# Attention weights requested a piece per half step, and an up projection of seven half-block products, in a hybrid encoder block

## The chip, the core and the metric

The kernel runs on one core of a Trainium2 chip. The metric is the device time in microseconds (us), the median of the runs. The engines have short names: PE multiplies matrices (PEld is its weight load, which overlaps), DVE is the vector engine, ACT the scalar engine, POOL is GpSimd, SP issues most DMAs. SBUF is the on-chip memory, PSUM holds what PE adds up, in banks of 128x512 float32.

## The reference

One layer on x of 1024 tokens by 1024 channels, float32. Two mixers read the normalised input; the second half is a gated feed-forward with a convolution of width 3 over the tokens:

```
proj = rmsnorm(x) @ w_in          # mLSTM q,k,v,o,gates; attention q,k,v; gates ga, gb
h_a  = mLSTM(both directions)     # 4 heads, chunks of 128 tokens
p    = softmax(q k^T)             # 8 heads of 2 x 64; weights p0 - lam * p1
h_b  = rmsnorm((p0 - lam*p1) @ v)
x    = x + (sigmoid(ga)*(h_a @ p_a) + sigmoid(gb)*(h_b @ p_b)) @ w_o
u    = conv3(rmsnorm(x) @ w_up) + conv_b      # 1024 x 5632
a, g = split(u)
x    = x + (gelu(g) * a) @ w_down             # 2816 x 1024
```

## The kernel before

**Products.** PE works in a short float32 format, so every matrix is split into a high half (a cast on ACT, L81) and a low half (a subtraction, L82, on DVE unless the caller names POOL), and each product is three matmuls: high by high, high by low, low by high (`mm3`, L112 to L114).

**Weights.** `wgran` brings 128x1024 numbers into `wraw`, a pool of one buffer (`NR = 1`), and splits them into `whi` and `wlo` (four buffers each). `load_w` does that for two such granules at once, where a set is asked for. All these DMAs are issued by SP.

**Order.** The program is written as Python loops; a scheduler with its own model of durations puts each engine's instructions into one fixed order, and semaphores hold an instruction until its inputs are there. An engine that waits holds all that stands behind.

**Stages**, by their times in the profile: the mLSTM to 445 us; attention, 445 to 1285; merge with p_a, p_b and w_o to 1547; feed-forward to the end.

**Attention** walks 32 steps (8 heads x 4 pairs of query blocks). `soft` (L645 to L657) makes scores, row maxima, exponentials `p` (ACT, L651) and subtracts the second softmax (DVE, L657). `av` transposes the weights (L677), splits them into `wTh` and `wTl`, and multiplies with v. Between these matmuls `filler(h, n)`, called for each of eight half steps n of a head, puts projections for later heads: q and k (`qk_piece`, L573 to L605), v, and the gates ga, gb (`gates`, ends with a tanh into `tg`, L162). It asks for the whole weight set at n = 2 (v, or the next gate set) and at n = 6 (q and k, two heads on). `kst` is a copy of the keys into the other half of the partitions, by DMA. `PRO` gate pieces are made before the first step, `LAST` says how many in the last head, `PA` how many blocks of h_a @ p_a are made there early.

**Norm and feed-forward.** `norm_transpose` (L206 to L217) scales a token half, transposes it on PE and splits it into `xn2`. For each of 22 column blocks j of 128, `up(j)` loads w_up's columns for a and g, multiplies (2 x 2 halves of tokens x 8 blocks of rows x 3 matmuls = 96 of 128x512) into PSUM tile `big`, and convolves from there: one ACT step (L936) and two of DVE (L937, L938); then gelu (L944), the product a*g (L946) and its split. After each pair of j, `down` multiplies the pair of before with w_down (96 matmuls) and adds into the eight resident tiles of x (L962, 16 adds of 128x512 a pair).

Of the kernel before, what the change touches and what calls it, by code (L numbers as in the profile page):

```python
# [10 lines left out]
F32 = mybir.dt.float32  # L11
F32R = mybir.dt.float32r
AF = mybir.ActivationFunctionType
ALU = mybir.AluOpType
# [30 lines left out]
TURN1 = {1: (1,)}  # L45

# [5 lines left out]
class Kern:  # L52
# [41 lines left out]

    def load_w(self, srcs, lo_eng=None):

        gr = []
        for g in range(2):
            loads, off = [], 0
            for s in srcs:  # L100
                n = s.shape[-1]
                loads.append((
                    lambda r, o=off, n=n: r.rearrange("p (k c) -> p k c", k=4)[:, :, o:o + n],
                    s[g * 512:(g + 1) * 512].rearrange("(k p) c -> p k c", p=P)))
                off += n
            hi, lo = self.wgran(loads, lo_eng)
            gr.append((hi.rearrange("p (k c) -> p k c", k=4), lo.rearrange("p (k c) -> p k c", k=4)))
        return lambda k: (gr[k // 4][0][:, k % 4], gr[k // 4][1][:, k % 4])

    def mm3(self, ps, a, b, start, stop):  # L110
        mm = self.nc.tensor.matmul
        mm(ps, a[0], b[0], start=start, stop=False)  # L112
        mm(ps, a[0], b[1], start=False, stop=False)  # L113
        mm(ps, a[1], b[0], start=False, stop=stop)  # L114

    def proj_cm(self, ps, w, c0, x, half):
        for _ in self.proj_cm_g(ps, w, c0, x, half):
# [25 lines left out]

    def gate_w(self, gg):
        if gg not in self.gst and gg < 8:
            off = (O_GA, O_GB)[gg // 4] + (gg % 4) * 256
            self.gst[gg] = self.load_w([self.I["w_in"][0][:, off:off + 256]])

    def gates(self, count, pool, ahead=False):
        for _ in range(count):  # L150
# [25 lines left out]
    def early_ya(self, tg, wide):  # L176
        m = self.ny
        self.ny += 1
        if m % 2 == 0:
            self.wpa = self.load_w([self.I["p_a"][0][:, m * P:m * P + 256]])  # L180
        self.nc.sync.dma_start(tg, self.sig_d[0][m * P:(m + 1) * P, :])
        ps = self.big() if wide else None
        for half in range(2):
            t = slice(half * 512, half * 512 + 512)
            pv = ps[:, t] if wide else self.small(tag="pj")
            yield from self.proj_cm_g(pv, self.wpa, (m % 2) * P, self.ha, half)
            self.nc.vector.scalar_tensor_tensor(tg[:, t], tg[:, t], 1.0, pv, op0=ALU.add, op1=ALU.mult)
        self.nc.sync.dma_start(self.ya_d[m * P:(m + 1) * P, :], tg)


def rstd_pow(K, out, ss, n, scr, width):
# [297 lines left out]
def attention(K, xn, hb_d):  # L489
# [3 lines left out]
    with tc.tile_pool(name="at", bufs=1, reuse_waits="tile") as ap, ExitStack() as es:  # L493
# [44 lines left out]
            while pend:  # L538
                tick()

        def load_v(hp):
            o = Obj()
            o.w = K.load_w([w_in[:, O_AV + hp * 256:O_AV + hp * 256 + 256]], G)
# [15 lines left out]
        def load_qk(h):  # L559
            o = Obj()  # L560
            o.w = K.load_w([w_in[:, O_AQ + h * 128:O_AQ + h * 128 + 128], w_in[:, O_AK + h * 128:O_AK + h * 128 + 128]], G)
            o.q, o.k, o.st = [], [], {}
            return o

# [69 lines left out]
        def soft(o, st, j):  # L634
# [12 lines left out]
            for c_ in range(2):  # L647
                sp = sps[c_]
                V.tensor_reduce(sm[:, c_:c_ + 1], sp, op=ALU.max, axis=AX.X, negate=True)  # L649
                p_ = ap.tile([P, 1024], F32, tag=f"p{c_}", bufs=3 - 2 * c_, name=K.nm("p"))  # L650
                A.activation(p_, sp, AF.Exp, bias=sm[:, c_:c_ + 1], accum_out=sm[:, 2 + c_:3 + c_])  # L651
                pt.append(p_)
            V.reciprocal(sm[:, 4:6], sm[:, 2:4])
            V.tensor_copy(st.inv[:, j:j + 1], sm[:, 4:5])
# [80 lines left out]
                        tick()  # L735

        on = vn = None

        def is_v(h):
            return h % 2 == 1 and h + 1 < AH  # L740
# [80 lines left out]
def merge_ffn(K, ha_d, hb_d, out):  # L821
    nc, tc, I = K.nc, K.tc, K.I
    V, G, A, T = nc.vector, nc.gpsimd, nc.scalar, nc.tensor
    with tc.tile_pool(name="mf", bufs=1, reuse_waits="tile") as fp, ExitStack() as es:
# [61 lines left out]
        xn, pw = None, []  # L886

        def pair(k):
            if k % 2 == 0:
# [16 lines left out]
            for bp in range(4):  # L906
                wo_piece(w, cg, bp * 2)
        ws = [wo(2), wo(3)]
        for half in range(2):
            for i in range(2):  # L910
                if half == 1 and i == NCG:
                    sp = [g4("nxs", tag="wk") for _ in range(2)] + [g4("nxs", tag="B") for _ in range(2)]
                    xn = h2("xn2", "B")
                    norm_transpose(K, lambda blk: acc[blk], xn, g2, fp, 0, lambda x: [sp.pop(0)] * 2, pair)
                for bp in range(2):
                    wo_piece(ws[i], 2 + i, half * 4 + bp * 2)
        norm_transpose(K, lambda blk: acc[blk], xn, g2, fp, 1, lambda x: [g4("nxs")] * 2, lambda k: K.small())
        ffn(K, fp, g4, acc, xn, out)


def ffn(K, fp, g4, acc, xn, out):
    nc, tc, I = K.nc, K.tc, K.I
    V, G, A, T = nc.vector, nc.gpsimd, nc.scalar, nc.tensor
    w_up, w_dn = I["w_up"][0], I["w_down"][0]
    cw = fp.tile([P, 3, 44], F32, tag="cw", name="cw")
    cb = fp.tile([P, 44], F32, tag="cb", name="cb")
    for t in range(3):
        nc.sync.dma_start(cw[:, t, :], I["conv_w"][0][t, 0].rearrange("(k p) -> p k", p=P))
    nc.sync.dma_start(cb, I["conv_b"][0].rearrange("(k p) -> p k", p=P))

    def conv(j, w, c0):
        u = K.big()
        for half in range(2):
            K.proj_cm(u[:, half * 512:half * 512 + 512], w, c0, xn, half)
        c = g4("cv")
        A.activation(c, u, AF.Identity, bias=cb[:, j:j + 1], scale=cw[:, 1, j:j + 1])  # L936
        V.scalar_tensor_tensor(c[:, 1:], u[:, :1023], cw[:, 0, j:j + 1], c[:, 1:], op0=ALU.mult, op1=ALU.add)  # L937
        V.scalar_tensor_tensor(c[:, :1023], u[:, 1:], cw[:, 2, j:j + 1], c[:, :1023], op0=ALU.mult, op1=ALU.add)  # L938
        return c

    def up(j):
        w = K.load_w([w_up[:, j * P:(j + 1) * P], w_up[:, DFF + j * P:DFF + (j + 1) * P]])
        g = conv(NFF + j, w, P)
        A.activation(g, g, AF.Gelu_apprx_tanh)  # L944
        a = conv(j, w, 0)
        V.tensor_tensor(a, a, g, op=ALU.mult)  # L946
        hh = g4("fhh", F32R)
        hl = g4("fhl", F32R)
        K.split(hh, hl, a)
        return hh, hl  # L950

    def down(j0, hs):
        ws = [K.wgran([(lambda r: r, w_dn[(j0 + i) * P:(j0 + i + 1) * P, :])]) for i in range(2)]
        last = j0 + 2 == NFF
        for blk in range(NB):
            t = slice(blk * P, (blk + 1) * P)
            for half in range(2):
                o = slice(half * 512, half * 512 + 512)
                ps = K.small()
                for i in range(2):  # L960
                    K.mm3(ps, (hs[i][0][:, t], hs[i][1][:, t]), (ws[i][0][:, o], ws[i][1][:, o]), i == 0, i == 1)
                V.tensor_tensor(acc[blk][:, o], acc[blk][:, o], ps, op=ALU.add)  # L962
                if last and blk == NB - 1:
                    nc.sync.dma_start(out[blk * P:, o], acc[blk][:, o])
            if last and blk < NB - 1:
                nc.sync.dma_start(out[blk * P:(blk + 1) * P, :], acc[blk])

    prev = None
    for j in range(0, NFF, 2):
        hs = [up(j), up(j + 1)]  # L970
        if prev is not None:
            down(*prev)
        prev = (j, hs)
    down(*prev)


@with_exitstack
# [62 lines left out]
```

## Time and profile before

| what | value |
|---|---|
| runs | 2294.85, 2299.35, 2299.68 us |
| median | 2299.35 us |
| profiled execution | 2291.85 us, its span 2290.1 us |
| mean granted PE clock | 0.986 |
| PE busy | 96% of the span |

The span runs from the first to the last instruction that the profiler shows; times in rows count from its start. Busy counts only time in which an instruction runs. A matmul's own duration overlaps the next one's, so the cost of one in a row of matmuls is read from a window with its count. The granted clock of 1.00 is 2.4 GHz, 0.5 is 1.2 GHz.

### The profile page before, as it was taken

How to read it: one execution, taken by the hardware profiler on the slowest of the kernel's cores; microseconds unless marked ns; L12 is line 12 of the kernel's file. 1: busy time of each engine (PE TensorE's matmuls, PEld its weight loads, DVE VectorE, ACT ScalarE, POOL GpSimd, SP SyncE). 2: the span in 40 equal slices, each digit the busy share in tenths (PEclk: the TensorE clock that was granted, in tenths of full speed). 3: DMA queues.
4: the chain of work that ended last, by engine and by line, in shares of the span. 5: the costliest groups of instructions: out<-in, count | busy, mean ns of one | idle time of the engine just before them, and what ended most of it. 6: DMA issues, size and time to landing. Idle time of an engine off the chain costs nothing.

```text
span 2290.1 us, 29966 instructions
## 1 busy us (share of the span) xinstructions
PE 2197.2 (96%) x12200; PEld 1888.8 (82%) x12200; DVE 1239.5 (54%) x2020; ACT 804.1 (35%) x1429; POOL 313.8 (14%) x298
## 2 busy tenths in 40 slices
PE   7999999989999899899999999999999999999999
PEld 6888888888789789798878778997888888888887
DVE  3455252358687686787755345244444444545455
ACT  4333232245455455555545222133222221222220
POOL 0131101233133141332300010000000000000000
PEclk9999999999999999999999999999999999999999
DMA  3123222221210311202232665111111111111112
GB/s 121 40 83 98 64 55 74 77 57 35 63 43 26 79 31 37 71 21 63 52 97 70 194 166 159 63 47 47 37 56 47 47 51 42 38 54 56 45 48 83
DMA packets 171307, 150.83 MB, mean 66 GB/s; under 512 B 37304, under 2 KB 153048, under 8 KB 171168
## 3 DMA queue, kind: packets, MB, share of 16 engines
q1 hardware_dynamic: 165616, 129.17, 20.2%
q0 software_dynamic: 5552, 19.73, 2.7%
q8 instruction: 96, 1.57, 0.3%
q14 instruction: 43, 0.35, 0.0%
HBM read 117.64 MB, written 22.84 MB: 61 GB/s over the span
## 4 chain that ended last, share of the span: by engine, by line
PE 76%; DMA 10%; DVE 6%; ACT 3%; issue 3%; POOL 2%; SPq 1%; ACTq 0%; POOLq 0%; DVEq 0%
PE pj L112 8%; PE pj L113 8%; PE pj L114 7%; PE big L114 7%; PE big L112 7%; PE big L113 7%; PE sm L112 6%; PE sm L113 6%; PE sm L114 6%; DMA wraw<-in_w_in_dram 6%; PE big L645 4%; PE pt L677 2%; ACT whi L81 2%; POOL wlo L82 1%; PE cr L435 1%
## 5 line engine op out<-in xcount | busy, mean ns | idle before, releaser
L81 ACT CAST whi<-wraw 128x1024 fp32r<-128x1024 f32 x156 | 163.7, 1049 | 596.0 <-PE sm L114 207.5
L82 DVE TENSOR_TENSOR wlo<-wraw,whi 128x1024 fp32r<-128x1024 f32 x132 | 162.5, 1231 | 372.2 <-ACT whi L81 372.1
L112 PE MATMUL pj<-whi,xn 128*128 128x256 f32 x960 | 277.6, 289 | 15.5 <-ACT whi L81 15.4
L112 PE MATMUL big<-xn2h,whi 128*128 128x512 f32 x704 | 278.2, 396 | 1.0 <-ACT xn2h L216 1.0
L114 PE MATMUL big<-xn2h,wlo 128*128 128x512 f32 x704 | 279.1, 396 | 0.0
L113 PE MATMUL big<-xn2l,whi 128*128 128x512 f32 x704 | 277.2, 394 | 0.8 <-DVE xn2l L217 0.8
L113 PE MATMUL pj<-wlo,xn 128*128 128x256 f32 x960 | 276.3, 288 | 0.5 <-POOL wlo L82 0.4
L114 PE MATMUL pj<-whi,xn 128*128 128x256 f32 x960 | 276.2, 288 | 0.0
L112 PE MATMUL pj<-xn,whi 128*128 128x512 f32 x512 | 212.6, 417 | 12.6 <-ACT xn L216 5.5
L114 PE MATMUL pj<-xn,wlo 128*128 128x512 f32 x512 | 209.0, 408 | 0.0
L113 PE MATMUL pj<-xn,whi 128*128 128x512 f32 x512 | 208.8, 408 | 0.0
L112 PEld LDWEIGHTS pj<-whi,xn 128*128 128x128 f32 x960 | 185.1, 193 | 19.5 <-ACT whi L81 17.3
L113 PEld LDWEIGHTS pj<-wlo,xn 128*128 128x128 f32 x960 | 185.0, 193 | 2.9 <-POOL wlo L82 1.3
L962 DVE TENSOR_TENSOR x<-x,sm 128x512 f32<-128x512 f32 x176 | 119.6, 686 | 122.9 <-PE sm L114 122.9
L114 PEld LDWEIGHTS pj<-whi,xn 128*128 128x128 f32 x960 | 185.0, 193 | 0.8
L651 ACT ACTIVATE p<-big,smx 128x1024 f32<-128x1024 f32 x128 | 143.2, 1120 | 89.2 <-DVE smx L649 72.8
L649 DVE TENSOR_REDUCE smx<-big 128x1 f32<-128x1024 f32 x128 | 154.3, 1217 | 36.9 <-PE big L645 36.5
L645 PE MATMUL big<-kst,qst 128*128 128x512 f32 x512 | 145.5, 410 | 16.6 <-DMA kst<-kst 12.0
L113 PEld LDWEIGHTS big<-xn2l,whi 128*128 128x128 f32 x704 | 132.2, 188 | 34.0 <-DVE xn2l L217 1.1
L112 PEld LDWEIGHTS big<-xn2h,whi 128*128 128x128 f32 x704 | 132.2, 188 | 32.4 <-ACT xn2h L216 1.2
L114 PEld LDWEIGHTS big<-xn2h,wlo 128*128 128x128 f32 x704 | 132.2, 188 | 32.1
L112 PE MATMUL sm<-whi,fhh 128*128 128x512 f32 x352 | 139.4, 396 | 0.0
(255 smaller groups left out, 4408.5 us busy)
## 6 DMA issues: line engine op xcount, KB each, us to landing
wraw<-in_w_up_dram SPq DMA_DIRECT2D x88, 256.0 KB, 3.2
wraw<-in_w_in_dram SPq DMA_DIRECT2D x40, 512.0 KB, 5.3
wraw<-in_w_in_dram SPq DMA_DIRECT2D x48, 256.0 KB, 4.5
wraw<-in_w_down_dram SPq DMA_DIRECT2D x22, 512.0 KB, 3.2
x<-in_x_dram SPq DMA_DIRECT2D x16, 512.0 KB, 4.7
sig<-tg SPq DMA_DIRECT2D x32, 256.0 KB, 2.4
kst<-kst SPq DMA_DIRECT2D x64, 128.0 KB, 2.4
tgl<-sig POOLq DMA_DIRECT2D x13, 512.0 KB, 4.5
```

Of the source, the lines that this page charges most:

```text
L81: self.nc.scalar.copy(hi, src)
L82: (lo_eng or self.nc.vector).tensor_tensor(lo, src, hi.bitcast(F32), op=ALU.subtract)
L112: mm(ps, a[0], b[0], start=start, stop=False)
L113: mm(ps, a[0], b[1], start=False, stop=False)
L114: mm(ps, a[1], b[0], start=False, stop=stop)
L435: T.matmul(nps[:, :MV + 1], pm[:, t], va[:, j, :], start=True, stop=i == 0)
L645: T.matmul(sps[c_][:, half * 512:half * 512 + 512], o.q[st.qp][:, c_, t], o.k[half][:, c_, s_, :], start=s_ == 0, stop=s_ == 1)
L649: V.tensor_reduce(sm[:, c_:c_ + 1], sp, op=ALU.max, axis=AX.X, negate=True)
L651: A.activation(p_, sp, AF.Exp, bias=sm[:, c_:c_ + 1], accum_out=sm[:, 2 + c_:3 + c_])
L677: T.transpose(pt[:, kk * 256 + j * P:kk * 256 + (j + 1) * P], st.w[j][:, kb * P:(kb + 1) * P], K.ident)
L962: V.tensor_tensor(acc[blk][:, o], acc[blk][:, o], ps, op=ALU.add)
```

## The change

**Attention.** A class `Weights` splits a set's life into `load(g)`, which requests one granule, and `make(g)`, which splits it. `filler` requests the first granule at n = 0, splits it and requests the second at n = 1, splits that at n = 2 and requests the next set, and so on. `make` is told to come after `K.mark`, the latest exponential. The low halves of all sets of `filler` are made on POOL, those of the gates too, which were on DVE. `PRO`, `LAST` and `PA` shift gate pieces to before the first step, and one more p_a block into the last head.

**Up.** A and B are each cut into 2 x 2 blocks (rows of the contraction, and token halves of A; the column blocks of a and g of B). Seven half-block products, in the manner of Strassen, replace eight: per j 7 x 4 x 3 = 84 matmuls in place of 96. Their operands are sums: `norm0` and `norm1` build S1 to S4 of the activations once, `prep` forms sums of weight blocks for each j (four DVE subtractions, seven splits with the low half on POOL). Partial results are joined by copies on ACT and adds on DVE into SBUF tiles `u`; the convolution reads these. a*g runs on POOL and goes to DRAM (`h_d`) by a POOL DMA. x goes to DRAM too (`x1_d`).

**Down** is a loop of its own behind up: for each token half 22 row blocks of w_down, 24 matmuls each, adding up in eight PSUM banks; h is read back and split, w_down is read twice, x is read back and added at the end of each half.

```diff
-NCG = 0
-PA = (0, 0, 0, 0, 0, 0, 0, 1)
-PRO = 2
-LAST = (2, 2, 2, 2, 2, 0, 0, 0)
+PA = (0, 0, 0, 0, 0, 0, 1, 1)
+PRO = 4
+LAST = (2, 2, 2, 2, 0, 0, 0, 0)
...
+class Weights:
...
+    def load(self, g):
+        K = self.K
+        self.raw = K.wp.tile([P, 1024], F32, tag="wraw", bufs=NR, name=K.nm("wraw"))
...
+    def make(self, g, after=None):
...
+            with K.tc.issue_after(after):
+                K.split(hi, lo, self.raw, self.lo_eng)
...
-            if n == 2 and not last:
-                if is_v(h):
-                    vn = load_v((h + 1) // 2)
-                else:
-                    K.gate_w(K.ng // 4)
-            if n == 6 and h + 2 < AH:
-                on = load_qk(h + 2)
+                if n == 0:
+                    wx = Weights(K, src_v((h + 1) // 2), G) if is_v(h) else Weights(K, K.gate_src(K.ng // 4), G)
+                    wts[0] = wx
+                    wx.load(0)
+                elif n == 1:
+                    wts[0].make(0, K.mark)
+                    wts[0].load(1)
+                elif n == 2:
+                    wts[0].make(1, K.mark)
...
+                    wts[1].load(0)
+                elif n == 4:
+                    wts[1].make(0, K.mark)
+                    wts[1].load(1)
+                elif n == 5:
+                    wts[1].make(1, K.mark)
...
+        def sums(kk):
+            V.tensor_tensor(a22, a21, a22, op=ALU.add)
+            V.tensor_tensor(a21, a11, a21, op=ALU.subtract)
+            V.tensor_tensor(a11, a22, a11, op=ALU.subtract)
+            V.tensor_tensor(a12, a12, a11, op=ALU.subtract)
+            for n, (name, v) in enumerate((("S2", a11), ("S1", a22), ("S3", a21), ("S4", a12))):
+                h, l = self.block(name, kk, "B" if kk >= 2 and n == 0 else "A")
+                K.split(h, l, v, G if n % 2 else V)
...
+    ORDER = (("X", "11", 0, 0), ("Y", "12", 0, 1), ("X", "S2", 1, 0), ("Z", "S1", 1, 1),
+             ("X", "S3", 2, 0), ("Z", "S4", 2, 1), ("X", "22", 3, 0))
...
+        pair(u["b11"], u["b21"])
+        V.tensor_tensor(t3, u["b22"], u["b12"], op=ALU.subtract)
+        V.tensor_tensor(u["b12"], u["b12"], u["b11"], op=ALU.subtract)
+        V.tensor_tensor(t2, u["b22"], u["b12"], op=ALU.subtract)
+        pair(t2, u["b12"])
+        pair(t3, u["b22"])
+        V.tensor_tensor(u["b21"], u["b21"], t2, op=ALU.subtract)
+        pair(u["b21"])
...
+        g = self.conv(u["ug"], NFF + j)
+        nc.scalar.activation(g, g, AF.Gelu_apprx_tanh)
+        a = self.conv(u["ua"], j)
+        nc.gpsimd.tensor_tensor(a, a, g, op=ALU.mult)
+        nc.gpsimd.dma_start(self.h_d[j * P:(j + 1) * P, :], a)
```

On DVE in the feed-forward, one column block before: `cv` is the convolution, read from PSUM tile `big`, `x` the resident sums, `sm` PSUM.

```order
L937 SCALAR_TENSOR_TENSOR cv_16350<-big_16301,cw,cv_16350 128x1023
L938 SCALAR_TENSOR_TENSOR cv_16350<-big_16301,cw,cv_16350 128x1023
L82 TENSOR_TENSOR wlo_16557<-wraw_16553,whi_16556 128x1024
L937 SCALAR_TENSOR_TENSOR cv_16404<-big_16355,cw,cv_16404 128x1023
L962 TENSOR_TENSOR x_2017_13273<-x_2017_13273,sm_16425 128x512
L962 TENSOR_TENSOR x_2017_13273<-x_2017_13273,sm_16433 128x512
L938 SCALAR_TENSOR_TENSOR cv_16404<-big_16355,cw,cv_16404 128x1023
```

And on DVE now, all of one column block: `ur` are raw weight blocks, `ut` their sums, `u` the joined result in SBUF.

```order
L1123 TENSOR_TENSOR ut_14957<-ur_14784,ur_14781 128x512
L1124 TENSOR_TENSOR ur_14781<-ur_14781 128x4x128
L1177 SCALAR_TENSOR_TENSOR cv_14912<-u_14749,cw,cv_14912 128x1023
L1125 TENSOR_TENSOR ut_14957<-ur_14784,ur_14781 128x512
L1178 SCALAR_TENSOR_TENSOR cv_14912<-u_14749,cw,cv_14912 128x1023
L1177 SCALAR_TENSOR_TENSOR cv_14917<-u_14748,cw,cv_14917 128x1023
L1130 TENSOR_TENSOR ur_14784<-ur_14784,ut_14957 128x4x128
L1178 SCALAR_TENSOR_TENSOR cv_14917<-u_14748,cw,cv_14917 128x1023
L1165 TENSOR_TENSOR u_14891<-sm_14875,z_14955 128x512
L1167 TENSOR_TENSOR u_14891<-sm_14929,s_14889 128x512
L1152 TENSOR_TENSOR u_15032<-sm_15018,s_15031 128x512
```

The low halves and a*g have left DVE; the convolution reads SBUF twice, and the weight subtractions are new. On POOL, which had no instruction in the feed-forward, one column block now (`ul` are low halves, `uh` high halves):

```order
L81 TENSOR_TENSOR ul_14907<-ur_14781,uh_14906 128x512
L81 TENSOR_TENSOR ul_14907<-ur_14784,uh_14906 128x512
L81 TENSOR_TENSOR ul_14962<-ut_14957,uh_14961 128x512
L81 TENSOR_TENSOR ul_14962<-ur_14781,uh_14961 128x512
L1186 TENSOR_TENSOR cv_14917<-cv_14917,cv_14912 128x1024
L1187 DMA h_d<-cv_14917 128x1024
L81 TENSOR_TENSOR ul_14994<-ut_14957,uh_14993 128x512
L81 TENSOR_TENSOR ul_14994<-ur_14784,uh_14993 128x512
L81 TENSOR_TENSOR ul_15014<-ur_14784,uh_15013 128x512
```

a*g stands behind four of the seven low halves of the next column block. On ACT in attention, the place of a weight cast before (`whi`), among work of the projections:

```order
L651 ACTIVATE p_5860,smx_5848<-big_5849,smx_5848 128x1024
L81 CAST wTh_5648<-pt_5643 128x512
L630 COPY kst_5738<-pt_5745 64x2x256
L81 CAST whi_5589<-wraw_5587 128x1024
L602 CAST st_5803<-raw_5726 128x2x2x64
L604 CAST st_5803<-raw_5726 128x2x128
```

And now, right behind the two exponentials of a step:

```order
L687 ACTIVATE p_6689,smx_6677<-big_6678,smx_6677 128x1024
L687 ACTIVATE p_6692,smx_6677<-big_6679,smx_6677 128x1024
L80 CAST whi_6723<-wraw_6605 128x1024
L733 COPY og_6580<-po_4234 128x256
L606 COPY raw_6665<-pj_6607 128x512
L638 CAST st_6648<-raw_6582 128x2x2x64
```

The cast keeps its kind and size; its place is tied to the exponentials.

## Rows read from the trace of the kernel before

**Rows 1.** Page, part 1: busy us (share of span) xinstructions, by engine

```profile
PE 2197.2 (96%) x12200; PEld 1888.8 (82%) x12200; DVE 1239.5 (54%) x2020; ACT 804.1 (35%) x1429; POOL 313.8 (14%) x298
```

**Rows 2.** Windows: stretch, us, busy of PE PEld DVE ACT POOL, PEclk, DMA, GB/s

```profile
1700.00:1800.00 100.00, 100.00 (x430) 80.47 (x429) 50.51 (x57) 20.48 (x19) 0.00 (x0) 1.00 0.14 43
505.00:1285.00 780.00, 730.40 (x4829) 657.90 (x4828) 556.61 (x971) 408.71 (x849) 203.16 (x163) 0.97 0.21 57
1552.00:2286.00 734.00, 733.60 (x3151) 590.26 (x3149) 354.19 (x374) 167.40 (x155) 0.00 (x0) 1.00 0.16 49
645.00:671.00 26.00, 20.31 (x148) 19.01 (x146) 22.80 (x38) 14.41 (x31) 14.48 (x10) 0.87 0.25 61
723.00:749.00 26.00, 26.00 (x213) 25.40 (x212) 24.41 (x45) 15.31 (x37) 15.80 (x14) 1.00 0.07 17
```

**Rows 3.** Page, part 5: count | busy us, mean ns | idle before

```profile
L112 PE MATMUL big<-xn2h,whi 128*128 128x512 f32 x704 | 278.2, 396 | 1.0 <-ACT xn2h L216 1.0
L112 PE MATMUL sm<-whi,fhh 128*128 128x512 f32 x352 | 139.4, 396 | 0.0
L962 DVE TENSOR_TENSOR x<-x,sm 128x512 f32<-128x512 f32 x176 | 119.6, 686 | 122.9 <-PE sm L114 122.9
```

**Rows 4.** Waits of PE, attention: us in total, times, longest

```profile
PE pj L112 <- ACT whi L81: 18.2, 8, 3.8
PE pt L677 <- DVE wTl L82: 14.4, 8, 4.1
PE big L645 <- DMA kst<-kst: 9.0, 3, 3.1
PE big L645 <- ACT p L651: 4.6, 5, 2.1
```

**Rows 5.** Timeline of ACT: start us, us, instruction [idle before <-releaser]

```profile
580.60 1.05 ACT L81 CAST whi<-wraw 128x1024 fp32r<-128x1024 f32 x1 [3.58 <-DMA wraw<-in_w_in_dram]
588.73 1.04 ACT L81 CAST whi<-wraw 128x1024 fp32r<-128x1024 f32 x1 [3.81 <-DMA wraw<-in_w_in_dram]
```

**Rows 6.** Source lines: count, ns min/median/max, first and last start, forms

```profile
L657 DVE SCALAR_TENSOR_TENSOR p<-p,smx,p x64: 1269/1284/3446, 508.3 to 1238.0; 128x1024 f32<-128x1024 f32 x64
L82 DVE TENSOR_TENSOR wTl<-pt,wTh x128: 673/684/696, 521.9 to 1275.5; 128x512 fp32r<-128x512 f32 x128
L82 POOL TENSOR_TENSOR wlo<-wraw,whi x24: 2345/2396/3406, 408.9 to 1091.1; 128x1024 fp32r<-128x1024 f32 x24
L82 DVE TENSOR_TENSOR wlo<-wraw,whi x18: 1218/1226/1228, 474.1 to 1263.7; 128x1024 fp32r<-128x1024 f32 x18
L573 POOL TENSOR_TENSOR raw<-raw,gq x32: 1266/1297/1859, 462.0 to 1130.2; 128x512 f32<-128x512 f32 x32
L598 DVE TENSOR_TENSOR raw<-raw,qss x32: 674/691/1777, 466.4 to 1140.2; 128x512 f32<-128x512 f32 x32
```

**Rows 7.** Timeline of POOL and DVE, columns as in rows 5

```profile
560.63 2.40 POOL L82 TENSOR_TENSOR wlo<-wraw,whi 128x1024 fp32r<-128x1024 f32 x1 [1.46 <-ACT whi L81]
560.67 3.45 DVE L657 SCALAR_TENSOR_TENSOR p<-p,smx,p 128x1024 f32<-128x1024 f32 x1
```

**Rows 8.** Lines by form: FFN, attention, first norm half; columns as rows 3

```profile
L944 ACT ACTIVATE cv<-cv 128x1024 f32<-128x1024 f32 x20 | 21.2, 1061 | 55.1 <-DVE cv L938 55.1
L81 ACT CAST wTh<-pt 128x512 fp32r<-128x512 f32 x128 | 73.1, 589 | 54.7 <-PE pt L677 43.7 <-PE po L114 10.5
L209 DVE TENSOR_SCALAR nxs<-x,nr 128x1024 f32<-128x1024 f32 x4 | 3.0, 751 | 1.3 <-POOL nr L194 1.3
```

**Rows 9.** Waits of PE after attention, columns as rows 4

```profile
PE big L112 <- ACT xn2h L216: 1.0, 1, 1.0
PE big L113 <- DVE xn2l L217: 0.8, 1, 0.8
```

**Rows 10.** Page, part 2: GB/s in 40 slices of the span

```profile
GB/s 121 40 83 98 64 55 74 77 57 35 63 43 26 79 31 37 71 21 63 52 97 70 194 166 159 63 47 47 37 56 47 47 51 42 38 54 56 45 48 83
```

**Rows 11.** Timeline of DVE, the last instruction, columns as rows 5

```profile
2285.64 0.69 DVE L962 TENSOR_TENSOR x<-x,sm 128x512 f32<-128x512 f32 x1 [0.71 <-PE sm L114]
```

More of the change, by code (lines that the diff above doesn't have):

```diff
@@ L95, in load_w, with mm3 @@
     def load_w(self, srcs, lo_eng=None):
-        gr = []
+        w = Weights(self, srcs, lo_eng)
         for g in range(2):
[L99 to L110, printed above, removed]
+            w.load(g)
+            w.make(g)
+        return w
+    def mm3(self, ps, a, b, start, stop, again=False):
         mm = self.nc.tensor.matmul
-        mm(ps, a[0], b[0], start=start, stop=False)
-        mm(ps, a[0], b[1], start=False, stop=False)
-        mm(ps, a[1], b[0], start=False, stop=stop)
+        mm(ps, a[0], b[0], start=start, stop=False, skip_group_check=again)
+        mm(ps, a[0], b[1], start=False, stop=False, skip_group_check=again)
+        mm(ps, a[1], b[0], start=False, stop=stop, skip_group_check=again)
     def proj_cm(self, ps, w, c0, x, half):
@@ L188, in early_ya, with __init__, __call__ @@
         self.nc.sync.dma_start(self.ya_d[m * P:(m + 1) * P, :], tg)
+class Weights:
+    def __init__(self, K, srcs, lo_eng=None):
+        self.K, self.srcs, self.lo_eng = K, srcs, lo_eng
+        self.raw, self.gr = None, []
+    def load(self, g):
+        K = self.K
+        self.raw = K.wp.tile([P, 1024], F32, tag="wraw", bufs=NR, name=K.nm("wraw"))
+        off = 0
+        for s in self.srcs:
+            n = s.shape[-1]
+            K.nc.sync.dma_start(self.raw.rearrange("p (k c) -> p k c", k=4)[:, :, off:off + n],
+                                s[g * 512:(g + 1) * 512].rearrange("(k p) c -> p k c", p=P))
+            off += n
+    def make(self, g, after=None):
+        K = self.K
+        hi = K.wp.tile([P, 1024], F32R, tag="whi", bufs=NH, name=K.nm("whi"))
+        lo = K.wp.tile([P, 1024], F32R, tag="wlo", bufs=NW, name=K.nm("wlo"))
+        if after is None:
+            K.split(hi, lo, self.raw, self.lo_eng)
+        else:
+            with K.tc.issue_after(after):
+                K.split(hi, lo, self.raw, self.lo_eng)
+        self.gr.append((hi.rearrange("p (k c) -> p k c", k=4), lo.rearrange("p (k c) -> p k c", k=4)))
+    def __call__(self, k):
+        h, l = self.gr[k // 4]
+        return h[:, k % 4], l[:, k % 4]
 def rstd_pow(K, out, ss, n, scr, width):
@@ L908, in merge_ffn @@
         ws = [wo(2), wo(3)]
-        for half in range(2):
-            for i in range(2):
[L911 to L938, printed above, removed]
-        return c
[L941 to L956, printed above, removed]
@@ new lines, in down @@
+def down(K, g4, up, out):
+    nc, V = K.nc, K.nc.vector
+    w_dn = K.I["w_down"][0]
+    for th in range(2):
+        ps = [[K.small() for _ in range(2)] for _ in range(4)]
+        tt = slice(th * 512, th * 512 + 512)
+        for kp in range(NFF // 2):
+            raw = g4("hr", tag="B")
+            nc.sync.dma_start(raw.rearrange("p (k t) -> p k t", k=2),
+                              up.h_d[kp * 256:(kp + 1) * 256, tt].rearrange("(k p) t -> p k t", p=P))
+            hh, hl = g4("hh", F32R), g4("hl", F32R)
+            K.split(hh, hl, raw)
+            for i in range(2):
+                k = kp * 2 + i
+                w = g4("wr", tag="B")
+                nc.sync.dma_start(w, w_dn[k * P:(k + 1) * P, :])
+                wh = K.wp.tile([P, 1024], F32R, tag="whi", bufs=NH, name=K.nm("dh"))
+                wl = K.wp.tile([P, 1024], F32R, tag="wlo", bufs=NW, name=K.nm("dl"))
+                K.split(wh, wl, w)
+                for b4 in range(4):
+                    t = slice(i * 512 + b4 * P, i * 512 + (b4 + 1) * P)
+                    for half in range(2):
+                        o = slice(half * 512, half * 512 + 512)
+                        K.mm3(ps[b4][half], (hh[:, t], hl[:, t]), (wh[:, o], wl[:, o]), k == 0, k == NFF - 1)
+        for b4 in range(4):
+            blk = th * 4 + b4
+            r = slice(blk * P, (blk + 1) * P)
+            x = g4("x1r", tag="acc")
+            nc.sync.dma_start(x, up.x1_d[r, :])
@@ L957, in down @@
             for half in range(2):
                 o = slice(half * 512, half * 512 + 512)
[L959 to L974, printed above, removed]
+                V.tensor_tensor(x[:, o], x[:, o], ps[b4][half], op=ALU.add)
+                if blk == NB - 1:
+                    nc.sync.dma_start(out[r, o], x[:, o])
+            if blk < NB - 1:
+                nc.sync.dma_start(out[r, :], x)
 @with_exitstack
```

216 lines of the change are left out of this document (208 added, 8 removed).

## Prediction, made before the changed kernel ran

> **What bounds the kernel now.** I read the page's busy line first: TensorE (PE) is busy for 96% of the span, the vector engine (DVE) for 54%, GpSimd (POOL) for 14% [rows 1]. A share that high says that the time moves with PE's work, or with holes torn in it; so the windows come next, stage by stage. In the feed-forward stretch PE has no hole: 733.60 of 734 us busy, granted clock 1.00, which is the 2.4 GHz level, and 100 us hold 430 of the 128x512 matmuls, so one costs 100/430 = 0.2326 us [rows 2]. Three products per block make 704x3 = 2112 of them for the up projection and 352x3 = 1056 for the down projection [rows 3]. In the attention stretch PE is busy for 730.4 of 780 us, at a mean clock of 0.97: some 50 us of holes [rows 2], and after the longer ones the lower clock level, as in the window with 0.87 [rows 2]. The waits name them: 18.2 us in 8 waits for ACT's cast of a weight granule, 14.4 us in 8 for the low half of transposed softmax weights, 9.0 for the key's DMA copy [rows 4]. ACT's timeline shows how the first arise: the cast stands in ACT's fixed order and itself waits for its DMA, 3.58 and 3.81 us [rows 5], with all later ACT work behind it.
>
> All sums below are made against the profiled execution, 2291.85 us (span 2290.1); the median of the runs, 2299.35, lies 7.5 us above it, and I add that at the end.
>
> **A. Matmuls removed.** Up: 84 matmuls for each of 22 column blocks j in place of 96, so 264 fewer, each on the path. 264 x 0.2326 = **-61.4 us**. Down keeps its 1056.
>
> **B. From w_o into up.** Before, PE loses 1.0 and 0.8 us here [rows 9]. Now norm1 must turn the second token half and build the sums S1 to S4 before products 2 to 5 can start. Behind the last w_o matmul DVE has 54 instructions: 36 with both inputs in SBUF (0.69 each by the 128x512 row of [rows 6], 24.8 us), 4 normalisations (0.75, [rows 8]), 9 reads of PSUM (0.69, like the adds of [rows 3]) and a few short ones: some 36 us if nobody disturbs it. POOL has 19 low halves of 128x512 at 1.27 and two DMA issues, some 25 us. PE has products 0 and 1 (24 matmuls), the products of a later start and 36 transposes in that time, at most 84 x 0.2326 + 4 = 23 us. How DVE and POOL share is the question. The trace has it: a two-input instruction of DVE on 128x1024 takes 1.269 us at least and 1.284 in the middle, but 3.446 once [rows 6], and that one started 0.04 us after a 2.40 us POOL instruction [rows 7]: DVE stood still until POOL had finished. Of 128 DVE instructions with one input in PSUM none took over 0.696 [rows 6]. So two-input work of DVE and POOL's work take turns. (The Trainium skill, "SBUF — State Buffer", section "Who interferes with whom", says the same as a rule: DVE's second SBUF input goes through an interface shared with GpSimd, the first to start holds it for the whole instruction. The trace agrees, 3.446 against 1.269. The rule speaks against this change, which sets POOL to work all through the up projection, where it was idle; with turns the sum is the one below, without them that of the first rival.) Taking turns wherever they meet, S1 and S2 are complete after about 50 us, so PE stands for 50 - 23 = 27 us instead of 1.8: **+25 us** (bounds +10 if they hardly meet, +30 if every POOL instruction comes first).
>
> **C. The steady up projection.** PE needs 84 x 0.2326 = 19.54 us per j. DVE's two-input instructions per j: four subtractions of weights (0.68) and four convolution steps, which read u from SBUF now instead of PSUM (1.28, the two-input row of 128x1024, [rows 6]): 7.84 us. POOL, which had nothing here (0.00 busy, [rows 2]): seven low halves (1.27) and the product a*g (2.35): 11.2 us. Turns alone make 19.1 us, just under PE's 19.54, and not all the rest hides: the second and third weight pairs can be built only after DVE's subtractions of the same j, and a*g only after gelu (1.06 on ACT, [rows 8]) and the convolution of a. Walking the rows of DVE and POOL once round with these hops I get 19.7 to 20.5 us per j; I take 20.2, so 0.7 x 21 = **+15 us** (bounds 0, PE covers it, and +50: hops of 2.3 us per j not covered). ACT has seven casts of 128x512 at 0.589 [rows 8], three copies, two convolutions and a gelu, under 12 us per j: not a bound. The three PSUM adds per j (0.69) read one SBUF input and meet nobody.
>
> **D. Down, apart.** PE's work is the same: 24 matmuls per weight row block, 5.58 us. Beside it ACT casts 128x1024 and half of an h block (about 1.6 us), DVE subtracts (about 1.8), both hidden; the 176 adds of 0.686 into x [rows 3] become 16. POOL is idle there. The DMA brings 768 KB per 5.58 us, 141 GB/s, where the kernel before has shown a slice of 194 [rows 10]: hidden. h goes through DRAM, but each load waits only for its own two blocks of h, long stored except the last. At the change of stage and between the halves PE may wait for banks to be read: **+2.5 us** (0 to +5).
>
> **E. The end.** Now the last thing is one add of 0.69 after the last matmul and the store [rows 11]. After: a half's eight adds follow the last row block's products bank by bank, three matmuls (0.70) to an add (0.69), so one or two stay behind the last matmul; but 2 MB of stores now start only then, 512 KB of it last: **+1 us** (0 to +5).
>
> **F. Attention.** With a piece of weights requested per half step, its DMA is landed before the cast comes up, and the cast stands right behind the exponential: the 18.2 us should go, and with them part of the 14.4 us, since wTh stands behind those held casts on ACT. Against it: the low half of the gate weights moves from DVE (1.226) to POOL (2.396, [rows 6]), 2.4 us during which the two-input DVE work (subtracting the second softmax, and the rope of q and k) stands; DVE is already busy 22.80 and 24.41 of 26 us in places [rows 2]. What the casts leave, the key's DMA (9.0) and p (4.6) are waited for still. I take **-15 us**, nearest the cast row (bounds -35: both rows go, and the low-clock stretches behind them; +5: the waits only change their names). One p_a weight set moves from merge into attention: 0.
>
> **Sum:** -61.4 + 25 + 15 + 2.5 + 1 - 15 = -32.9, so 2259 for an execution like the profiled one, and with the 7.5 us **2266 us** for the median. Its own range is 2240 to 2288.
>
> **Rivals.** *First: the turns cost little.* Instructions meet less often than I count, since each engine waits for ACT and PE between them: transition +12, steady 0, attention -20, D and E 3.5: -65.9, which gives 2233. For it: DVE was 24.41 and POOL 15.80 busy of 26 us at a PE without a hole [rows 2]. Against: much of that DVE work reads PSUM. *Second: attention gives nothing.* The waits move to wTl and the key's copy, since DVE is the engine that is nearly full there: -17.9, which gives 2281. For it: DVE's 22.80 of 26 in a window with holes. Against: ACT's casts held others visibly [rows 5]. *Third, slower: the shared interface decides the up projection.* If DVE and POOL run strictly one after the other, with PE's hand-over between (an add that reads PSUM, a cast) never covered, a j takes 19.1 + some 2.8 us of hops = 21.9: 2.3 x 22 = +50, transition +30, D and E 3.5, attention -5: +17, which gives 2316; holes of 2 us per j could bring the lower clock level besides. It turns the sign from about 1.5 us per j on (21.0). For it: the sum of turns is 98% of PE's time, so any hop shows. Against: two-thirds of the hops lie a whole j ahead of their use, because weights are prepared for j + 1.
>
> **Chances.** Forecast 0.47, first rival 0.20, second 0.17, third 0.16. No change is told from noise here within 0.2%, 4.6 us (the three runs spread over 4.83). Faster by more than that: the first three, less the upper edge of the second: 0.79. Within: 0.06, between the second and third. Slower: 0.15. The range for 8 in 10: from below the first rival's time, attention at its -35, to the point between the second and third: 2222 to 2302.
>
> **What will show it.** A: 84 matmuls of 128x512 per j in the up window. B: a hole of 20 to 30 us behind the last w_o matmul, PE waiting for S1 or S2; under 12 the first rival. C: spacing of the h stores 20.2 us, waits on POOL's low halves or on DVE's steps, with L1177/L1178 lengthened from 1.28 to 2.5 and more beside POOL; 19.6 speaks for the first rival, 21 and more for the third. F: the row of PE waits for whi in attention gone, wTl under 14.4. I am wrong in mechanism if DVE's two-input steps are not lengthened in the up projection, if PE waits for ACT or DMA there, or if down runs over 5.7 us per row block.

## The result and the profile after

The changed kernel takes 2235.01 us (median of 4 runs, 2233.91 to 2236.34) against 2297.1 for the kernel before in the same comparison: ratio 0.9737, 95% interval 0.9707 to 0.9767. The forecast was 2266, its range 2222 to 2302, so the direction and the range held. The profiled execution is one of 2236.34 us; its span of 2234.6 is 55.5 us under that of before, where the forecast had 32.9.

The page's busy line after, same columns as [rows 1]:

```profile
PE 2136.8 (96%) x11936; PEld 1834.9 (82%) x11936; DVE 1303.3 (58%) x1986; ACT 912.0 (41%) x1659; POOL 680.5 (30%) x529
```

12200 - 11936 = 264 matmuls are gone, as counted. POOL has doubled its share. To split the 55.5 us into what lies before the feed-forward and what lies in it, PE's timeline serves: the last w_o matmul and the first of up. First the kernel before, then after (start, duration, instruction):

```profile
1539.32 0.28 PE L114 MATMUL sm<-whi,yl 128*128 128x256 f32 x1
1539.79 0.50 PE L112 MATMUL big<-xn2h,whi 128*128 128x512 f32 x1
```

```profile
1507.14 0.28 PE L107 MATMUL sm<-whi,yl 128*128 128x256 f32 x1
1510.18 0.50 PE L105 MATMUL sm<-A,uh 128*128 128x512 f32 x1 [2.32 <-ACT uh L80]
```

The w_o product ends 1539.3 - 1507.1 = 32.2 us earlier; from there to the end it is 2290.1 - 1539.3 = 750.8 before and 2234.6 - 1507.1 = 727.5 after, 23.3 less. Windows of the changed kernel, columns as in [rows 2]: attention, transition, up with the start of down, down:

```profile
505.00:1285.00 780.00, 751.15 (x4970) 674.18 (x4969) 561.28 (x976) 410.43 (x856) 240.88 (x177) 0.99 0.25 66
1507.00:1571.00 64.00, 45.53 (x172) 33.36 (x171) 54.37 (x63) 29.06 (x50) 39.23 (x31) 0.81 0.21 66
1571.00:1990.00 419.00, 411.67 (x1752) 328.83 (x1751) 297.01 (x231) 198.38 (x293) 277.58 (x181) 1.00 0.29 98
1990.00:2228.00 238.00, 238.00 (x1017) 191.35 (x1016) 82.23 (x74) 59.76 (x59) 3.85 (x2) 1.00 0.37 130
```

PE's idle time in attention's 780 us fell from 49.6 to 28.9, and the mean clock rose from 0.97 to 0.99. The transition (1507 to 1571) has holes of 18.5 us and a mean clock of 0.81; the up loop has 7.3 us of holes in 419; down has none. PE's longest waits, in attention and behind it, columns as in [rows 4]:

```profile
PE pt L713 <- DVE wTl L81: 13.6, 9, 2.5
```

```profile
PE sm L105 <- ACT AS L80: 11.0, 4, 5.0
PE sm L105 <- ACT s L1159: 4.1, 4, 3.1
PE sm L105 <- DVE u L1165: 3.1, 2, 1.6
```

The row for the weight cast `whi`, 18.2 us in [rows 4], does not come up any more. Behind attention PE waits for the casts of the sums S (`AS`), and in the loop for a copy (`s`) and an add (`u`).

### The profile page after: what moved, and what is told of

Read it like the earlier page. It is cut to its first block, busy times and chain, and to the rows that moved or that the text cites. A ratio compares the mean times of both kernels' runs of the same rounds, so it can differ in the third digit from the quotient of the medians.

```text
span 2234.6 us, 30400 instructions
## 1 busy us (share of the span) xinstructions
PE 2136.8 (96%) x11936; PEld 1834.9 (82%) x11936; DVE 1303.3 (58%) x1986; ACT 912.0 (41%) x1659; POOL 680.5 (30%) x529
## 3 DMA queue, kind: packets, MB, share of 16 engines
q1 hardware_dynamic: 175296, 156.96, 24.5%
## 4 chain that ended last, share of the span: by engine, by line
PE 70%; DVE 13%; DMA 6%; issue 4%; ACT 4%; POOL 2%; SPq 0%; DVEq 0%; ACTq 0%; POOLq 0%
PE sm L105 11%; PE sm L106 11%; PE sm L107 11%; PE pj L105 8%; PE pj L106 7%; PE pj L107 7%; DMA wraw<-in_w_in_dram 3%; PE big L681 3%; PE pt L713 2%; DVE smx L685 2%; DVE p L693 1%; PE cr L465 1%; PE cr L470 1%; PE cr L467 1%; PE po L106 1%
## 5 line engine op out<-in xcount | busy, mean ns | idle before, releaser
L81 POOL TENSOR_TENSOR ul<-ur,uh 128x512 fp32r<-128x512 f32 x110 | 173.3, 1592 | 38.4 <-ACT uh L80 38.4
L105 PEld LDWEIGHTS pj<-whi,xn 128*128 128x128 f32 x960 | 181.9, 189 | 3.2 <-ACT kT L300 0.3
L107 PEld LDWEIGHTS pj<-whi,xn 128*128 128x128 f32 x960 | 181.7, 189 | 1.0
L80 ACT CAST whi<-wraw 128x1024 fp32r<-128x1024 f32 x88 | 92.2, 1048 | 216.5 <-DMA wraw<-in_w_in_dram 103.1
L81 DVE TENSOR_TENSOR wlo<-wraw,whi 128x1024 fp32r<-128x1024 f32 x54 | 67.6, 1251 | 168.3 <-ACT whi L80 168.3
L105 PE MATMUL sm<-AS,uh 128*128 128x512 f32 x352 | 140.5, 401 | 15.9 <-ACT AS L80 11.0
L106 PE MATMUL sm<-AS,uh 128*128 128x512 f32 x352 | 141.3, 401 | 0.6 <-POOL AS L81 0.6
L107 PE MATMUL sm<-AS,ul 128*128 128x512 f32 x352 | 140.7, 401 | 0.0
L106 PE MATMUL sm<-dl,hh 128*128 128x512 f32 x352 | 139.5, 396 | 0.0
L105 PE MATMUL sm<-dh,hh 128*128 128x512 f32 x352 | 139.0, 396 | 0.0
L107 PE MATMUL sm<-dh,hl 128*128 128x512 f32 x352 | 138.9, 396 | 0.0
L224 POOL TENSOR_TENSOR inv<-inv,mhalf 128x2 f32<-128x2 f32 x32 | 23.0, 718 | 366.9 <-DVE inv L223 308.5
```

The costliest lines, as they stand in the source:

```text
L80: self.nc.scalar.copy(hi, src)
L81: (lo_eng or self.nc.vector).tensor_tensor(lo, src, hi.bitcast(F32), op=ALU.subtract)
L105: mm(ps, a[0], b[0], start=start, stop=False, skip_group_check=again)
L106: mm(ps, a[0], b[1], start=False, stop=False, skip_group_check=again)
L107: mm(ps, a[1], b[0], start=False, stop=stop, skip_group_check=again)
L224: K.nc.gpsimd.tensor_tensor(out, scr, K.mhalf[:scr.shape[0], :width], op=ALU.pow)
```

## The experiments

Twelve kernels, each with runs of the kernel before on the same chip. A ratio is against these, with its 95% interval behind it; an interval of 0.0045 is 10 us wide. First the halves apart.

**Attention alone.** The changed attention (every hunk of the diff but those of `merge_ffn`), the old feed-forward.

> The changed attention with the old feed-forward. Theory (attention gave 32 us: about 21 us fewer idle us of PE and about 11 us less of the lower clock level; the feed-forward gave the other 24): 2265 us, ratio 0.986, PE busy about 751 of 780 us in the attention stretch, mean clock 0.99. Rival (attention gave the forecast 15, the feed-forward the rest): 2282, ratio 0.9935.

2259.42 us, ratio 0.9837 (0.9815 to 0.9860); its profiled span of 2257.2 is 32.9 us under before's. The theory's size holds, the rival's 15 us does not: attention gave more than twice the forecast.

**Feed-forward alone.** The old PRO, LAST, PA in the changed kernel, and the old filler, whose lines stand in the next diff.

> The old attention with the changed feed-forward. Theory (the feed-forward's balance is -24: -61.6 of matmuls, +26 at the transition, +11 in the loops, +1 at the end): 2273 us, ratio 0.990; h stores 19.9 us apart. Rival (the interface shared by DVE and POOL costs little, feed-forward -47): 2250, ratio 0.980.

2265.82 us, ratio 0.9864 (0.9839 to 0.9890): between the two, nearer the theory in time. The span is 27.5 us under before's. The cast that opens the last merge block (`yh`) starts 4.0 us earlier than before (1443.8 against 1447.8) although attention is the old one; behind it 23.5 us are gained, the theory's number. PE still waits 18.4 us for whi. The two halves' gains add up to 72 us by the medians and 60 by the spans, where the whole change gives 62 and 56; the intervals, some 5 us either way each, allow for that.

**What in attention gave it.** The old filler again, but the new numbers.

```diff
-                if n == 0:
-                    wx = Weights(K, src_v((h + 1) // 2), G) if is_v(h) else Weights(K, K.gate_src(K.ng // 4), G)
...
+            if n == 2 and not last:
+                if is_v(h):
+                    vn = load_v((h + 1) // 2)
+                else:
+                    K.gate_w(K.ng // 4)
+            if n == 6 and h + 2 < AH:
+                on = load_qk(h + 2)
```

> The changed kernel with the old filler (whole sets requested at n = 2 and n = 6, gates' low halves on DVE), but with the new PRO, LAST and PA. Theory (most of attention's gain comes from requesting pieces ahead): 2255 to 2265 us, with the row of PE waiting for whi still there at 10 us or more. Rival (the new counts alone move each gate pair behind one weight set and so remove the waits): 2235 to 2240, no whi row.

2235.94 us, ratio 0.9733 (0.9709 to 0.9757). My theory fell, the rival is right: without pieces requested ahead, without the cast behind the exponential, and with the gates' low halves on DVE, the time is that of the whole change. So the new numbers are enough. What the new code would give with the old numbers was not run. PE's two largest waits in this kernel's attention; whi is not among the others either, and wTl is down to 0.7:

```profile
PE pt L713 <- DVE kst L666: 10.0, 5, 5.1
PE big L681 <- ACT p L687: 6.0, 5, 3.2
```

**The cast's place.** `make(g, K.mark)` becomes `make(g)`, in all four places.

```diff
-                    wts[0].make(0, K.mark)
+                    wts[0].make(0)
```

> The changed kernel without the instruction to place the casts behind the latest exponential; requests as in the changed kernel. Theory (the early request does the work, the cast's place decides only whether ACT stands before an exponential): 2235 to 2242 us, whi waits under 3 us. Rival (the place behind the exponential does the work): 2250 or more, whi waits back at 10 us or more, ACT casts idle over 3 us for their DMA.

2238.28 us, ratio 0.9737 (0.9711 to 0.9763): whi is not among PE's waits. With the new numbers, the place does nothing that can be measured.

**Two numbers in the kernel before.**

```diff
-PRO = 2
-LAST = (2, 2, 2, 2, 2, 0, 0, 0)
+PRO = 4
+LAST = (2, 2, 2, 2, 0, 0, 0, 0)
```

> The kernel before with two numbers changed: PRO 4 and LAST (2,2,2,2,0,0,0,0), PA and all code as before. Theory, formed after the run with the new counts alone: with PRO 2 the count of gate pieces stands at 2 beyond a multiple of 4 when an even head's n = 2 asks for a gate set, so it asks for the set that is there, and the next one is loaded on demand two pieces later; with PRO 4 it asks for the next one in time. So the whi row goes (18.2 to 0), the lower clock level with it, and about 30 us: 2265 to 2270, ratio 0.986 to 0.988. Rival (the moved p_a block or the new code shares the gain): 2275 to 2290.

2271.33 us, ratio 0.9879 (0.9860 to 0.9897), whi gone from PE's waits: 28 us, a little under the theory's 30. PE's idle time in attention's 780 us is 34.7 us and the mean clock 0.98, between before (49.6, 0.97) and after (28.9, 0.99), for waits on `kst` (7.8) and `p` (6.7) have grown.

The code says what the numbers change. `gates` works through sets of four pieces, and an even head's filler asks at n = 2 for set `K.ng // 4`, the number of pieces done by four. With two pieces made ahead, this is the set already in use; the next is loaded only when its first piece comes up, and its last two pieces are made two heads later. With four, each set is asked for, used and done with in one head.

The theory's load on demand is the smaller part of it. Of the eight waits in the kernel before, only two (at 589.8 and 777.6 us, 3.0 of the 18.2 us) are for a gate set. The other six, 15.2 us, come for the second granule of the set of v or of q and k. There the cast of the first granule waits for PE's last product with the set before, and only behind the split can `wraw` take the second granule, whose cast waits for the DMA. PE waited 1.67 us for the cast of the second row:

```profile
649.30 1.05 ACT L81 CAST whi<-wraw 128x1024 fp32r<-128x1024 f32 x1 [1.03 <-PE pj L114]
658.33 1.04 ACT L81 CAST whi<-wraw 128x1024 fp32r<-128x1024 f32 x1 [2.26 <-DMA wraw<-in_w_in_dram]
```

Meanwhile a gate set lies half used: it was cast at 580.6 and 588.7, its last products run from 750.2 to 767.4, and it holds two of the four `whi` buffers. That this is why the first granule's cast must wait is read from the code and agrees with the run; more buffers with the old numbers, which would show it, were not tried.

**And PA.** The same with `PA = (0, 0, 0, 0, 0, 0, 1, 1)`.

> The kernel before with PRO 4, LAST (2,2,2,2,0,0,0,0) and PA (0,0,0,0,0,0,1,1), its code untouched. Theory (the changed attention's gain is all in these numbers; PA's extra block fills holes in the last head and saves a weight set in merge): 2258 to 2263 us, as the whole changed attention gave with the old feed-forward (2259.4). Rival (the pieces requested ahead give the rest): 2268 to 2273, as with PRO and LAST alone.

2265.18 us, ratio 0.9867 (0.9843 to 0.9892): between the two, and its interval reaches both neighbours. Its profiled span is 2258.7 against 2257.2 for the whole changed attention and 2270.6 with PRO and LAST alone, which speaks for the theory; the medians don't decide it, so up to 6 us may belong to the new code.

**More work for POOL in up.** One low half made twice, so 22 more instructions of 1.27 us.

```diff
         pair(t3, u["b22"])
+        h, l = u["w"][-1]
+        G.tensor_tensor(l[:, :512].rearrange("p (k c) -> p k c", k=4), t3, h[:, :512].rearrange("p (k c) -> p k c", k=4).bitcast(F32), op=ALU.subtract)
```

> The changed kernel with one low half per column block (t3) made twice on POOL: 22 more instructions of 128x512 with two SBUF inputs, 1.27 us each. Theory (turns at the shared interface fill 19.1 us of a block in which PE needs 19.6, so little room is left): the h stores move from 19.9 to 20.4 us apart or more, +10 to +20 us, 2245 to 2255. Rival (DVE and POOL meet less than counted, PE alone sets the pace): 2233 to 2239, spacing 19.9 to 20.0.

2246.76 us, ratio 0.9778 (0.9763 to 0.9792), 11.8 us over the changed kernel. The h stores, of the changed kernel and of this one (ns min/median/max, first and last start):

```profile
L1187 POOL DMA_DIRECT2D h_d<-cv x22: 594/594/616, 1583.2 to 2002.0; - x22
```

```profile
L1189 POOL DMA_DIRECT2D h_d<-cv x22: 594/594/616, 1584.0 to 2013.6; - x22
```

(2002.0 - 1583.2)/21 = 19.94 us a block against 20.46: 0.5 of each added 1.27 us shows. The result is as the theory has it; the loop had little room left. In 17 of the blocks a step of the convolution (1.28 us by itself) now takes 3.4 to 8.6 us beside POOL, 7.96 of them at 1686.2, where POOL runs six instructions in a row; gelu waits for it, a copy stands behind gelu on ACT, and PE waits for the copy.

**Low halves of S on DVE.**

```diff
-                K.split(h, l, v, G if n % 2 else V)
+                K.split(h, l, v, V)
```

> The changed kernel with the low halves of S1 and S4 on DVE (0.69 each) instead of POOL (1.29 each), so all 16 on DVE: eight instructions moved. Theory (in the transition DVE's work and the turns that it loses to POOL add up): DVE gains 5.5 us of work and loses the turns beside eight POOL instructions, the time stays within 3 us of 2235. Rival (DVE's own work alone sets the transition, turns cost nothing): +5 us, 2240.

2235.13 us, ratio 0.9728 (0.9710 to 0.9745): no change. That the rival's +5 does not come agrees with turns being given back for the added work: in the 64 us behind the last w_o matmul DVE is busy for 54.7 us against 54.3, though 5.5 us of work came to it.

**Transition steps on ACT.**

```diff
-            nc.vector.tensor_scalar(o, x, r, None, op0=ALU.mult)
+            if half:
+                nc.scalar.activation(o, x, AF.Copy, scale=r)
+            else:
+                nc.vector.tensor_scalar(o, x, r, None, op0=ALU.mult)
...
-                V.tensor_scalar(f2[:, t], ps, self.g2[:, k:k + 1], None, op0=ALU.mult)
+                if i == 0:
+                    nc.scalar.activation(f2[:, t], ps, AF.Copy, scale=self.g2[:, k:k + 1])
+                else:
+                    V.tensor_scalar(f2[:, t], ps, self.g2[:, k:k + 1], None, op0=ALU.mult)
...
-                    V.tensor_tensor(self.b22[1], f2[:, t], self.b22[0].bitcast(F32), op=ALU.subtract)
+                    V.scalar_tensor_tensor(self.b22[1], ps, self.g2[:, k:k + 1], self.b22[0].bitcast(F32), op0=ALU.mult, op1=ALU.subtract)
```

> The changed kernel with DVE relieved in the transition: the four normalisations of the second half (0.75, up to 1.76 beside POOL) and four copies of transposed blocks out of PSUM (0.74) move to ACT, and four low halves read PSUM instead of a second SBUF tile. Theory (DVE, without a gap over 0.5 us from 1525 to 1558, sets the transition): 5 to 8 us less, 2227 to 2230. Rival (the chain from transposition to sum to split sets it, whoever does the steps): 2234 to 2238.

2231.22 us, ratio 0.9711 (0.9692 to 0.9729): 3.8 us under the changed kernel, a little short of the theory. The interval overlaps that of the changed kernel; the traces are clearer. PE's waits for `AS` fall from 11.0 to 4.8 us, and from up's first matmul to the third block's PE takes 64.3 us against 69.4, and three other kernels with the changed kernel's code in this stretch lie between 68.5 and 69.9: 5 us, the theory's lower edge.

**The same, and a*g on DVE.**

```diff
-        nc.gpsimd.tensor_tensor(a, a, g, op=ALU.mult)
+        nc.vector.tensor_tensor(a, a, g, op=ALU.mult)
```

> The changed kernel with the transition steps on ACT as in the run before and the product a*g on DVE (1.22 us) instead of POOL (2.40). Theory (per block the turns at the shared interface fall from 19.1 to 17.9 us, PE needs 19.6, and the waits left in the loop are for ACT and DVE steps, 7.9 us in all): spacing of the h stores 19.7 to 19.8, 2 to 5 us below the run with the transition alone, 2226 to 2229. Rival (PE is bound by itself there already): 2230 to 2233.

2224.18 us, ratio 0.9679 (0.9662 to 0.9696): 7.0 us further, more than expected, and with an interval wholly below that of the changed kernel; it touches that of the run before. The traces decide between these two: from up's first matmul to down's first 448.1 us against 459.8. The product itself takes 2.17 us on DVE (the middle of 22; 1.21 at least), not 1.22, since it meets POOL too. The up loop's window, in this kernel and in the one with more work for POOL:

```profile
1571.00:1990.00 419.00, 418.90 (x1796) 336.71 (x1795) 340.21 (x261) 203.62 (x298) 230.38 (x160) 1.00 0.33 112
```

```profile
1571.00:1990.00 419.00, 405.60 (x1710) 321.56 (x1709) 331.67 (x224) 193.68 (x288) 290.75 (x200) 0.99 0.28 90
```

PE's holes in this window: 13.4 us with more on POOL, 7.3 in the changed kernel, 0.1 with 2.4 us less on POOL and 1.2 more on DVE. That POOL's work tears the holes is shown. It is not the sum of the turns: over all blocks DVE's two-input steps exceed their own time by 4.4 us a block in the changed kernel, by 6.3 with more on POOL, and by 5.0 here, where PE has no hole. What a*g costs as a turn, by its place in POOL's order and by what the scheduler then puts elsewhere was not separated.

**Transition on ACT, low halves of S on DVE.**

> The changed kernel with the transition steps on ACT and all low halves of S1 to S4 on DVE. Theory (with DVE relieved, what remains are the turns with POOL): 1 to 4 us below the run with the steps on ACT alone, 2227 to 2230. Rival (DVE's own work is still the bound): 2232 to 2236.

2231.20 us, ratio 0.9709 (0.9690 to 0.9728): no change to the run with the steps on ACT, between both expectations; it decides nothing.

**Weight sums of block 1 later.** On top of the 2224 us kernel; the mark is the last sum of the activations, and the fourth subtraction follows the three.

```diff
-        V.tensor_tensor(t3, u["b22"], u["b12"], op=ALU.subtract)
-        V.tensor_tensor(u["b12"], u["b12"], u["b11"], op=ALU.subtract)
-        V.tensor_tensor(t2, u["b22"], u["b12"], op=ALU.subtract)
+        with K.tc.issue_after(self.mark) if u["j"] == 1 else ExitStack():
+            V.tensor_tensor(t3, u["b22"], u["b12"], op=ALU.subtract)
+            V.tensor_tensor(u["b12"], u["b12"], u["b11"], op=ALU.subtract)
+            V.tensor_tensor(t2, u["b22"], u["b12"], op=ALU.subtract)
```

> The kernel with the transition steps on ACT and a*g on DVE (2224 us), with DVE's weight subtractions of the second column block placed behind the last sum of the activations instead of ahead of the first. Theory (the four subtractions and their turns with POOL take DVE from 1520.7 to 1525.7 and hold an add that PE's transposes wait for): the sums come about 5 us earlier, 2217 to 2221. Rival (the second block's weights are then late, and PE waits for them at its third product): 2223 to 2230, with waits on ut's low halves behind the first block.

2225.40 us, ratio 0.9680 (0.9660 to 0.9699): the rival's time, but not its reason. DVE is relieved and the last low half of S is made 44.5 us behind the last w_o matmul in place of 48.1, but the third block begins no earlier (64.4 us from up's first matmul, 64.2 before). The waits for low halves of weights got shorter (1.9 us against 3.4), not longer; PE now waits 2.6 us for a low half of S and 0.9 for a copy instead of the 2.6 for the add.

## Why the prediction was right, and where it was not

The direction was sure from A alone. Of the 31 us between 2266 and 2235, 23 are in the sum, 17 of them in F; the rest is the step from the profiled execution to the median, +7.5 in the forecast and -1.3 here.

**A, matmuls removed: right.** 264 by the count of the page, at the price of the window.

**B, transition: right, +25 forecast, about +27 measured.** By PE's order 132 matmuls and 36 transposes lie in the window of 64 us; at 0.233 and about 0.12 they would take 35 (0.12 is an estimate: eight transposes in a row took 1.09 us in the run with the steps on ACT, the last one's end included), so 29 are lost against 1.8 before. I had it as a hole of 27 us; it is 18.5 us of holes and some 10 at the lower clock level behind them (0.81 in the row). The sums come about as forecast (S1 and S2 after 50 us): the last low half of an S is done 52.3 us behind the last w_o matmul. The turns are there too, in the transition and in the loop: DVE's first subtraction per block starts beside POOL and stands. The distribution of that line, of its neighbour and of the convolution step, in the changed kernel (ns min/median/max):

```profile
L1123 DVE TENSOR_TENSOR ut<-ur,ur x22: 680/3002/5511, 1510.2 to 1947.9; 128x512 f32<-128x512 f32 x22
L1124 DVE TENSOR_TENSOR ur<-ur x22: 675/1640/1777, 1510.9 to 1950.9; 128x512 f32<-128x512 f32 x22
L1177 DVE SCALAR_TENSOR_TENSOR cv<-u,cw,cv x44: 1269/1284/2396, 1567.1 to 1995.7; 128x1023 f32<-128x1023 f32 x44
```

One such case, and what hangs on it (the POOL row holds four instructions; the others are DVE, ACT and PE):

```profile
1785.10 5.03 POOL L81 TENSOR_TENSOR ul<-ur,uh 128x512 fp32r<-128x512 f32 x4
1785.17 5.51 DVE L1123 TENSOR_TENSOR ut<-ur,ur 128x512 f32<-128x512 f32 x1 [3.60 <-POOL ul L81]
1795.16 1.06 ACT L1184 ACTIVATE cv<-cv 128x1024 f32<-128x1024 f32 x1 [7.92 <-DVE cv L1178]
1796.74 0.51 PE L105 MATMUL sm<-AS,uh 128*128 128x512 f32 x1 [3.12 <-ACT s L1159]
```

DVE's 0.69 us became 5.51, nearly POOL's 5.03 on top. I had counted one turn of 1.27 at a meeting; here DVE stands for four of POOL's instructions in a row, and the 3.0 in the middle of the row above is a stand beside two. It isn't always so: at 1773.98 a subtraction gets in after one (L1130, 1.78 us). The convolution stands behind that subtraction on DVE, gelu (L1184) waits for it, the copy `s` stands behind gelu on ACT, and PE waits 3.12 us for the copy, the largest hole of the loop.

The sign that I named was L1177 and L1178, lengthened to 2.5. Of their 88 instructions 31 are, to between 1.7 and 2.4; the others keep about 1.28 (1.39 at most), and the subtractions take the larger part of the blow.

**C and D, loops: +17.5 forecast, about +10 measured.** The holes up to 1990 are 7.3 us, and none follow. A hole costs more than itself: the window of 419 us holds 1752 matmuls, and 1796 in the kernel with a*g on DVE, which has 0.1 us of holes. The 44 that are missing are 10 us at 419/1796 = 0.233; I put the other 3 down to the slow first matmul behind a hole (0.51 in the row) and the lower clock level behind the largest (0.89 from 1790 to 1800). So 84 matmuls take 20.1 us, against 20.2 forecast and 19.6 without holes. (The stores, at 19.94, don't stand in one place of PE's blocks.) The number was near; the picture of an even stretch was not: by PE's timeline 12 of the 19 blocks from the third on take 19.6 us, six take 20.0 to 21.4, and the one with the case above 24.5. What a turn costs depends on what stands behind it; only 0.5 us of each 1.27 added to POOL is passed on. Down loses nothing.

**E, the end: +1 forecast.** From the last matmul to the end 4.8 us against 4.5.

A to E sum to -61.4 + 27 + 10 + 0.3 = -24, the span says -23.3. Forecast was -17.9.

**F, attention: the step that failed.** Forecast -15, measured -32.2 up to the end of w_o (2.8 of it lie ahead of attention's first scores, where the kernels scatter by 4), of which 20.8 are idle time of PE in attention's window. The size was off because the sum had the cast row alone and nothing for the lower clock behind the removed waits, which was left to the bound of -35; the mean clock of that window rose from 0.97 to 0.99. The signs didn't tell: whi is gone, but wTl, which was to shrink with it, stands at 13.6 against 14.4. Worse, the reason was wrong: I put the gain down to pieces requested ahead and the cast behind the exponential, and called PRO, LAST and PA shifts of pieces. With the new numbers and the old code all of the gain is there, within the interval; in the kernel before, two numbers alone give 28 of the 33 to 39 us. The rows had shown eight waits for whi, and casts that waited for their own DMA [rows 5]. I asked how to bring these loads earlier, not why just these eight came late.

**The rivals.** The first came out nearest in time (2233), but for another reason: it had transition +12 and attention -20, where the runs show +27 and -32. The third, slower, needed 1.5 us a block more than the forecast's PE time; 0.5 came.

## What to carry to other kernels

When a few of many like transfers come late, first look for the count that puts their request behind their use; with two numbers changed the waits went here, and the new class for requests added nothing that could be measured to the new numbers. Ask too what a set that is kept half used takes from the others. Where an engine that was idle is given work, price what it holds from its neighbour, and follow what stands behind: a two-input step of DVE stood for as long as POOL ran on, up to 5.5 us for 0.69, and moving a*g from POOL to DVE gave 7 us. What PE loses at a change of stage is the hole and the slow stretch behind it.

## What was not expected of the hardware

A DVE step with one SBUF input can stand beside POOL too. The normalisation (L1024, one tile and a scalar per partition) took 0.751 us before [rows 8], and 1.76 here in two of its eight instructions, in a stretch where POOL ran (DVE, then POOL):

```profile
1516.96 1.76 DVE L1024 TENSOR_SCALAR nxs<-x,nr 128x1024 f32<-128x1024 f32 x1
```

```profile
1516.82 1.35 POOL L81 TENSOR_TENSOR ul<-ur,uh 128x512 fp32r<-128x512 f32 x1
```

The Trainium skill, "SBUF — State Buffer", section "Who interferes with whom", has it: a tensor_scalar may run in a mode that uses both port pairs, and then it contends as a two-input step does. The 1.0 us added here agrees; which mode the step ran in, no trace shows. Its cost by itself was not tried; in the run with transition steps on ACT it went together with others.
